# Rotary products and sums and the gate-merge additions on the vector engine instead of POOL

## The chip, the cores and the metric

The kernel runs on one core of one Trainium2 chip. The metric is the device time of one execution in microseconds (us). Before the change three timed runs gave 715.38, 715.96 and 716.66 us; the median is 715.96 us. The engines are named as the profile names them: PE is TensorE (matmul), PEld its weight loads, DVE the vector engine, ACT the scalar engine, POOL is GpSimd, SP the engine whose queue starts the DMA transfers.

## The reference, cut to what matters

One encoder layer over 512 tokens of width 1024, all in float32. A projection of the input gives queries, keys and values of two attention branches, and two sets of gate logits. Branch A is attention with a position bias. Branch B is differential attention, and its queries and keys (512 columns each) are first rotated:

```python
def partial_rope(t, cos, sin):            # the first 16 of each 64 columns
    t1 = t[..., :8]; t2 = t[..., 8:16]
    return concat([t1 * cos - t2 * sin, t1 * sin + t2 * cos, t[..., 16:]])

gates = sigmoid(g + b_gate);  g_a, g_b = split(gates)
merged = g_a * (o_a @ w_branch_a) + g_b * (o_b @ w_branch_b)
x = layer_norm(ALPHA * x + merged @ w_out)            # LN1
x = layer_norm(ALPHA * x + relu(x @ w_ff1)**2 @ w_ff2)  # LN2
```

## The kernel before

Every float32 product is made of three TensorE matmuls. Each operand is split in a high part (ACT casts it, line 84) and a low part (DVE subtracts the high part from the operand, line 85); high by high, high by low and low by high are summed in PSUM. The inner lines of this are L184 to L186 (`tmm`) and L189 to L191 (`smm`). Weights come in chunks of 128x1024 through a ring of three `raw` tiles; the ring parts `wh` and `wl` are the high and the low part.

The program is a generator, `proj()`, for the projections, which is advanced a step at a time between the units of the attention: 32 units of branch A (`attn_a`: 8 heads by 4 query blocks t), then those of branch B (`attn_b`). A unit of branch A computes scores (L275, L276) into one of three PSUM banks called `st`, DVE adds the bias and takes the maximum (L283) and so empties the bank, ACT takes the exponential (L285), POOL divides by the sum (L378, a TENSOR_SCALAR). Three units later PE transposes the result (L294) into another `st` bank, which ACT (L302) and DVE (L303) read into `pq`. The transposes of a unit take the bank from which L283 has just read the scores of the unit before, so PE can't go on until that L283 is done.

While branch A runs, the generator projects the queries and keys of branch B, head by head. `evac_qkb` copies the result to a tile `t` (128x512, called G in the profile, rows are columns of the projection), four small DMAs copy its rotated rows into `other` with the halves exchanged, and `rope` finishes the rotation of the tile before: `other` times the sine table (L500), `t` times the cosine table (L501), then the sum (L502), each over 80 rows and 512 columns. There are eight such tiles. In `prep_b` the rotated tile is split (L259 on ACT, L260 on DVE).

After branch B, `branch(1, ...)` multiplies the attention output by `w_branch_b` in eight groups. Each is scaled by its gate on DVE (L610), added to the same columns of branch A (L613), halved and split (L615 on ACT, L616 on DVE) into `mh` and `ml`. The two halves of `w_out` follow (`s_group`, four chunks of weights each), whose left operands are `mh` and `ml`; DVE adds the result to the input (L821), takes the statistics (L825), and LN1 of each block of 128 rows (L886 to L892) makes the tile that PE transposes (L903). Meanwhile DVE forms sums of blocks of the second MLP weight (L716), whose G tiles are loaded (L779) into buffers that the gates leave. The MLP follows, to the end of the program.

A scheduler sets the order of the instructions on each engine. Each engine works through its own list in order and waits where an operand isn't there. An instruction inside `tc.keep_in_program_order` is pinned: it keeps its place in the program.

Of the kernel before, what the change touches and what calls it, by code (L numbers as in the profile page):

```python
# [13 lines left out]
ALU = mybir.AluOpType  # L14
# [26 lines left out]
def block_kernel(ctx, tc, w, w2, x_t, x, pos, relb, bgate, lq1, lk1, lq2, lk2, subg,  # L41
                 ln1_g, ln1_b, ln1_gt, ln1_bt, ln2_g, ln2_b, out):
    nc = tc.nc
    V, A, G, T = nc.vector, nc.scalar, nc.gpsimd, nc.tensor
# [7 lines left out]
    def name(s):  # L52
        counter[0] += 1
        return f"{s}{counter[0]}"

    def xt(dt=F32):
        return big.tile([P, S], dt, tag="X", bufs=16, name=name("X"))
# [9 lines left out]
    def mm_bank():  # L67
        tag = rotation.pop(0)
        rotation.append(tag)
        return bank(tag)  # L70
# [80 lines left out]
    def chunk(ahead=2):  # L151
        c = next_chunk[0]
        prefetch(c + ahead + 1, c + max(ahead, 1))
        next_chunk[0] += 1
        return parts.pop(c)
# [27 lines left out]
    def tmm(ps, lw_h, lw_l, rh, rl, first, last):  # L183
        T.matmul(ps, lw_h, rh, start=first, stop=False)  # L184
        T.matmul(ps, lw_h, rl, start=False, stop=False)  # L185
        T.matmul(ps, lw_l, rh, start=False, stop=last)  # L186
# [205 lines left out]
    sin_t = tables.tile([P, S], F32, name="sin_t")  # L392
# [85 lines left out]
    def evac_qkb(which):  # L478

        def f(ps):  # L480
            t, o = gt(), other[len(qb[0] + qb[1]) % 2]
            A.activation(t, ps, AF.Copy, scale=0.125 if which == 0 else 1.0)
            for m in (0, 64):
                nc.sync.dma_start(out=o[m:m + 8], in_=t[m + 8:m + 16])
                nc.sync.dma_start(out=o[m + 8:m + 16], in_=t[m:m + 8])
            qb[which].append(t)
            turns.append((t, o))
            if len(turns) > 1:
                rope(*turns.pop(0))
        return f  # L490
# [6 lines left out]

    def rope(t, o):
        r = slice(0, 80)
        tc.keep_in_program_order(G.tensor_tensor(out=o[r], in0=o[r], in1=sin_t[r], op=ALU.mult))  # L500
        V.tensor_tensor(out=t[r], in0=t[r], in1=cos_t[r], op=ALU.mult)  # L501
        G.tensor_tensor(out=t[r], in0=t[r], in1=o[r], op=ALU.add)  # L502

    def prep_b(h):
        if turns:
            rope(*turns.pop())
        q1, k1 = (stack(qb[which][h], 1.0) for which in range(2))
        return q1, [swapped(q) for q in q1], k1
# [88 lines left out]
    def branch(b, oh, ol):  # L597

        for ip in range(4):
            wh, wl = chunk()  # L600
            for j in range(2):
                i = 2 * ip + j
                ps = mm_bank()
                for k in range(4):
                    off = k * 256 + j * 128
                    sl = slice(off % 512, off % 512 + 128)
                    tmm(ps, wh[off // 512][:, sl], wl[off // 512][:, sl], oh[k], ol[k],
                        k == 0, k == 3)
                g, m = gates[8 * b + i], gates[i]
                V.scalar_tensor_tensor(out=g, in0=g, scalar=1.0, in1=ps,  # L610
                                       op0=ALU.add, op1=ALU.mult)
                if b == 1:
                    G.tensor_tensor(out=m, in0=m, in1=g, op=ALU.add)  # L613
                    h, l = xt(FR), xt(FR)
                    A.activation(h, m, AF.Copy, scale=0.5)  # L615
                    V.scalar_tensor_tensor(out=l, in0=m, scalar=0.5, in1=h.bitcast(F32),  # L616
                                           op0=ALU.mult, op1=ALU.subtract)
                    mh.append(h)
                    ml.append(l)
                yield  # L620
# [10 lines left out]
    def proj():  # L631
        def before(c):
            for k in (2 * c + 2, 2 * c + 3):
                if 0 < c and k < KD:
                    load_x(k)
            if c > 1:
                for k in (2 * c, 2 * c + 1):
                    split_x(k)
        yield from s_group(xh, xl, evac_va, before)
        for p in range(4):  # L640
            yield from t_pair(xh, xl, [evac_qk(p, 0), evac_qk(p, 1)])
        for h in range(4):
            yield from t_pair(xh, xl, [evac_qkb(0), evac_qkb(1)])
        yield from s_group(xh, xl, evac_vb)
        for i in range(8):
            yield from t_pair(xh, xl, [evac_gate(i), evac_gate(8 + i)])
        yield from branch(0, oa_h, oa_l)
# [163 lines left out]
    for n, _ in enumerate(branch(1, ob_h, ob_l)):  # L811
        qt.load_next(2)
# [182 lines left out]
    for q in range(4):  # L995
# [24 lines left out]
        if last:  # L1020
            t, p3h, p3l = (late.tile([P, 4, S], dt, tag="x1t", bufs=4, name=name("x1t"))
                           for dt in (F32, FR, FR))
# [148 lines left out]
```

## Time and profile before

| | |
|---|---|
| timed runs | 715.38, 715.96, 716.66 us; median 715.96 us |
| profiled execution | 715.14 us, of which the span from first to last instruction 712.9 us |
| PE busy | 698.0 us (98%), 3259 matmuls |
| DVE busy | 535.7 us (75%), 1016 instructions |
| ACT busy | 383.3 us (54%), 700 instructions |
| POOL busy | 100.7 us (14%), 107 instructions |
| granted TensorE clock | 0.994 (mean of the span) |

The profiled execution's own time is its span and 2.2 us around it. The busy share is a mean over the span; how long a stage lasts is read from the engine that is never idle in it.

### The profile page before, as it was taken

To read this page: it belongs to the slowest core of one execution; us is meant where nothing else is said; L and a number is where in the kernel's file an instruction comes from. 1 tells how busy PE (TensorE), PEld (TensorE's weight loads), DVE (VectorE), ACT (ScalarE), POOL (GpSimd) and SP (SyncE) were. 2 spreads that over 40 slices of the span, in tenths; PEclk is the share of its full clock that TensorE was granted. 3 is DMA by queue.
4 is the path that set the end of the run, shared out by engine and by line. 5 is a ranking of instruction groups with operands and counts; after the bars stand their busy time and mean duration, and the time that the engine had idled before them with its cause. 6 is when DMAs were issued, how large, how long until landed. Compare 5 with 4: busy or idle time off the path is not lost.

```text
span 712.9 us, 9510 instructions
## 1 busy us (share of the span) xinstructions
PE 698.0 (98%) x3259; PEld 580.8 (81%) x3259; DVE 535.7 (75%) x1016; ACT 383.3 (54%) x700; POOL 100.7 (14%) x107
## 2 busy tenths in 40 slices
PE   9999999999999999999999999999999999999993
PEld 6888888888888888888889888888888888888883
DVE  6667668775667676669996898767894779956798
ACT  6556556644667666323556665166623675156610
POOL 2022266740111211034000000000000000000001
PEclk9999999999999999999999999999999999999997
DMA  8554232332333113176542247233640356220403
GB/s 299 209 154 123 95 85 83 111 93 89 93 103 101 59 60 118 60 261 228 189 140 68 89 133 245 66 119 115 214 144 31 117 174 202 68 89 1 148 8 110
DMA packets 36816, 87.27 MB, mean 122 GB/s; under 512 B 5665, under 2 KB 6433, under 8 KB 36769
## 3 DMA queue, kind: packets, MB, share of 16 engines
q1 hardware_dynamic: 36048, 85.72, 37.2%
q10 hardware_dynamic: 720, 0.95, 0.4%
q8 instruction: 25, 0.41, 0.2%
q14 instruction: 23, 0.18, 0.1%
HBM read 79.84 MB, written 2.10 MB: 115 GB/s over the span
## 4 chain that ended last, share of the span: by engine, by line
PE 88%; DVE 5%; ACT 2%; POOL 2%; issue 1%; DMA 1%; SPq 0%; DVEq 0%
PE mm L184 9%; PE mm L186 9%; PE mm L185 9%; PE st L184 6%; PE st L186 6%; PE st L185 6%; PE st L191 4%; PE st L190 4%; PE st L189 4%; PE mm L191 4%; PE mm L190 4%; PE mm L189 4%; PE o L184 2%; PE o L185 2%; PE o L186 2%; POOL G L613 2%
## 5 line engine op out<-in xcount | busy, mean ns | idle before, releaser
L85 DVE TENSOR_TENSOR wl<-raw,wh 128x1024 fp32r<-128x1024 f32 (+1 forms) x86 | 105.0, 1222 | 34.1 <-ACT wh L84 34.1
L84 ACT CAST wh<-raw 128x1024 fp32r<-128x1024 f32 (+1 forms) x86 | 88.5, 1029 | 65.8 <-PE mm L185 23.4
L184 PE MATMUL mm<-X,wh 128*128 128x512 f32 x256 | 103.2, 403 | 0.0
L186 PE MATMUL mm<-X,wl 128*128 128x512 f32 x256 | 100.0, 391 | 0.0
L185 PE MATMUL mm<-X,wh 128*128 128x512 f32 x256 | 99.9, 390 | 0.0
L84 ACT CAST V<-G 128x512 fp32r<-128x512 f32 x104 | 61.6, 619 | 45.2 <-DVE G L716 23.5
L186 PE MATMUL st<-x1t,wl 128*128 128x512 f32 (+1 forms) x200 | 76.2, 381 | 0.0
L185 PE MATMUL st<-x1t,wh 128*128 128x512 f32 (+1 forms) x200 | 76.1, 381 | 0.0
L184 PE MATMUL st<-x1t,wh 128*128 128x512 f32 (+1 forms) x200 | 75.9, 381 | 0.0
L85 DVE TENSOR_TENSOR V<-G,V 128x512 fp32r<-128x512 f32 x104 | 71.2, 697 | 3.1 <-ACT V L84 3.1
L186 PEld LDWEIGHTS mm<-X,wl 128*128 128x128 f32 x256 | 48.1, 188 | 10.5
L184 PEld LDWEIGHTS mm<-X,wh 128*128 128x128 f32 x256 | 48.2, 188 | 8.8
L285 ACT ACTIVATE e<-e,s 128x128 f32<-128x128 f32 (+3 forms) x64 | 36.0, 563 | 36.0 <-DVE s L283 35.2
L185 PEld LDWEIGHTS mm<-X,wh 128*128 128x128 f32 x256 | 48.3, 189 | 8.6
L869 POOL TENSOR_SCALAR s<-s 128x1 f32<-128x1 f32 x1 | 0.4, 411 | 370.9 <-DVE s L853 370.9
L716 DVE TENSOR_TENSOR G<-G,G 128x512 f32<-128x512 f32 x64 | 44.9, 721 | 6.2 <-DMA G<-in_w_dram 6.1
L378 POOL TENSOR_SCALAR e<-e,s 128x128 f32<-128x128 f32 (+3 forms) x32 | 36.7, 1146 | 65.4 <-DVE s L287 61.6
L189 PE MATMUL st<-V,X 128*128 128x512 f32 x116 | 45.3, 391 | 0.0
L190 PE MATMUL st<-V,X 128*128 128x512 f32 x116 | 45.2, 390 | 0.0
L191 PE MATMUL st<-V,X 128*128 128x512 f32 x116 | 45.2, 390 | 0.0
L185 PEld LDWEIGHTS st<-x1t,wh 128*128 128x128 f32 x200 | 37.6, 188 | 7.1
L186 PEld LDWEIGHTS st<-x1t,wl 128*128 128x128 f32 x200 | 37.6, 188 | 7.1
(268 smaller groups left out, 1575.1 us busy)
## 6 DMA issues: line engine op xcount, KB each, us to landing
raw<-in_w_dram SPq DMA_DIRECT2D x86, 512.0 KB
G<-in_w_dram SPq DMA_DIRECT2D x96, 256.0 KB
q<-q SPq DMA_DIRECT2D x32, 128.0 KB
G<-in_relb_dram SPq DMA_DIRECT2D x8, 256.0 KB
x<-in_x_dram SPq DMA_DIRECT2D x4, 512.0 KB
e<-in_x_t_dram SPq DMA_DIRECT2D x7, 256.0 KB
raw<-in_w_dram SPq DMA_DIRECT2D x4, 256.0 KB
out_dram<-x SPq DMA_DIRECT2D x3, 256.0 KB
```

Source lines behind the costliest of these rows:

```text
L84: A.copy(out=h, in_=src)
L85: i = (eng or V).tensor_tensor(out=l, in0=src, in1=h.bitcast(F32), op=ALU.subtract)
L184: T.matmul(ps, lw_h, rh, start=first, stop=False)
L185: T.matmul(ps, lw_h, rl, start=False, stop=False)
L186: T.matmul(ps, lw_l, rh, start=False, stop=last)
L189: T.matmul(ps, ah, w_h, start=first, stop=False)
L190: T.matmul(ps, ah, w_l, start=False, stop=False)
L191: T.matmul(ps, al, w_h, start=False, stop=last)
L285: A.activation(e[:, :n], e[:, :n], AF.Exp, bias=nm, scale=-1.0, accum_out=sums)
L378: G.tensor_scalar(ex[:, :n], ex[:, :n], r, None, op0=ALU.mult)
L613: G.tensor_tensor(out=m, in0=m, in1=g, op=ALU.add)
L716: V.tensor_tensor(out=out, in0=a, in1=b, op=ALU.subtract)
```

## The change

The two rotary operations on POOL go to DVE, and the first loses its pin. The addition in the gate merge goes to DVE.

```diff
     def rope(t, o):
         r = slice(0, 80)
-        tc.keep_in_program_order(G.tensor_tensor(out=o[r], in0=o[r], in1=sin_t[r], op=ALU.mult))
+        V.tensor_tensor(out=o[r], in0=o[r], in1=sin_t[r], op=ALU.mult)
         V.tensor_tensor(out=t[r], in0=t[r], in1=cos_t[r], op=ALU.mult)
-        G.tensor_tensor(out=t[r], in0=t[r], in1=o[r], op=ALU.add)
+        V.tensor_tensor(out=t[r], in0=t[r], in1=o[r], op=ALU.add)
...
                 if b == 1:
-                    G.tensor_tensor(out=m, in0=m, in1=g, op=ALU.add)
+                    V.tensor_tensor(out=m, in0=m, in1=g, op=ALU.add)
```

POOL loses 24 instructions (8 of L500, 8 of L502, 8 of L613), DVE gets 24. PE's list is the same, row by row. The lists of DVE, ACT and SP change order around the moved operations.

On DVE in branch A, at the third of the eight rotations (G_1194; a unit with t = 0 follows), the list changes as follows. L363 reads the attention output, L260 splits the first rotated tile, V_1262 is a low part of that output, e_1289 are the scores that PE waits to have read.

```order
 L85 TENSOR_TENSOR wl_1305<-raw_1146,wh_1304 128x1024
 L287 RECIPROCAL s_1242<-s_1239 128x1
+L500 TENSOR_TENSOR other_99<-other_99,sin_t 80x512
+L363 TENSOR_TENSOR e_1100<-o_1250,e_1100 64x512
 L501 TENSOR_TENSOR G_1194<-G_1194,cos_t 80x512
-L363 TENSOR_TENSOR e_1100<-o_1250,e_1100 64x512
 L260 SCALAR_TENSOR_TENSOR q_1776<-G_1038,q_1776 64x512
-L260 SCALAR_TENSOR_TENSOR q_1779<-G_1038,q_1779 64x512
 L85 TENSOR_TENSOR V_1262<-e_1100,V_1261 128x512
+L502 TENSOR_TENSOR G_1194<-G_1194,other_99 80x512
 L283 ISA e_1289,s_1290<-st_1286,G_429 128x128
```

L500 and L502 now stand ahead of L283, and the second L260 has gone behind it. The seventh rotation (G_1515) has the same change.

On ACT in the gate merge, the list around the cast of the fourth chunk of `w_out` (wh_3487, from raw_3471) changes as follows. V_3433 and V_3434 are casts of the next chunk, raw_3473.

```order
+L615 ACTIVATE X_3425<-G_2981 128x512
+L84 CAST wh_3487<-raw_3471 128x1024
 L84 CAST V_3514<-G_3304 128x512
-L615 ACTIVATE X_3425<-G_2981 128x512
 L84 CAST V_3433<-raw_3473 128x512
-L84 CAST wh_3487<-raw_3471 128x1024
 L84 CAST V_3434<-raw_3473 128x512
```

The cast of the fourth chunk now stands ahead of that of the fifth, no longer behind it.

On DVE, at the end of the first half of `w_out`, the additions of the result (L821, to x_0 to x_3) and the statistics (L825) are now spread between the splits of the last weights (V_3444 to V_3876).

```order
 L85 TENSOR_TENSOR V_3444<-raw_3477,V_3442 128x512
+L821 SCALAR_TENSOR_TENSOR x_0_3210<-x_0_3210,mm_3449 128x512
 L85 TENSOR_TENSOR V_3447<-raw_3479,V_3445 128x512
+L825 BN_STATS bn_3590<-x_0_3210 128x6
+L821 SCALAR_TENSOR_TENSOR x_1_3211<-x_1_3211,mm_3450 128x512
 L85 TENSOR_TENSOR V_3448<-raw_3479,V_3446 128x512
+L825 BN_STATS bn_3599<-x_1_3211 128x6
+L821 SCALAR_TENSOR_TENSOR x_2_3212<-x_2_3212,mm_3451 128x512
+L821 SCALAR_TENSOR_TENSOR x_3_3213<-x_3_3213,mm_3452 128x512
+L825 BN_STATS bn_3612<-x_2_3212 128x6
+L825 BN_STATS bn_3621<-x_3_3213 128x6
 L85 TENSOR_TENSOR V_3876<-G_3408,V_3875 128x512
```

The same eight rows stood behind V_3876 and one L716. The next row in both lists is the L821 of the second half (x_0 from o_3623), with which LN1 of the first row block begins, so the same work stands ahead of it as before, and the L613 besides.

## Rows read from the trace of the kernel before

**Rows 1.** The page's head, and PE's busy tenths in 40 slices of the span.

```profile
span 712.9 us, 9510 instructions
...
PE   9999999999999999999999999999999999999993
```

**Rows 2.** Busy time by window: window, its length, then the named engines.

```profile
320.00:357.00 37.00, 36.94 (x164) 30.27 (x163) 35.24 (x49) 15.94 (x23) 8.37 (x5) 1.00 0.63 209
```

**Rows 3.** Timeline, PE at 114 and 129 us: start, duration, what.

```profile
114.17 0.28 PE L276 MATMUL st<-q,q 128*128 128x256 f32 x1
115.02 0.52 PE L294 MATMUL st<-ident,e 128*128 128x128 f32 x3 [0.57 <-DVE s L283]
...
129.53 0.28 PE L276 MATMUL st<-q,q 128*128 128x256 f32 x1
129.65 0.49 PE L294 MATMUL st<-ident,e 128*128 128x128 f32 x3
```

**Rows 4.** Timeline, DVE from 109 to 115 us.

```profile
109.03 0.69 DVE L501 TENSOR_TENSOR G<-G,cos_t 80x512 f32<-80x512 f32 x1
109.75 0.68 DVE L363 TENSOR_TENSOR e<-o,e 64x512 f32<-64x512 f32 x1
110.47 0.69 DVE L260 SCALAR_TENSOR_TENSOR q<-G,q 64x512 fp32r<-64x512 f32 x1
...
111.19 1.78 DVE L260 SCALAR_TENSOR_TENSOR q<-G,q 64x512 fp32r<-64x512 f32 x1
113.00 1.67 DVE L85 TENSOR_TENSOR V<-e,V 128x512 fp32r<-128x512 f32 x1
114.59 0.28 DVE L283 CUSTOM_DVE_ANT_0 e<-st,G 128x128 f32<-128x128 f32 x1
```

**Rows 5.** Timeline, POOL from 109 to 114 us.

```profile
109.25 1.91 POOL L378 TENSOR_SCALAR e<-e,s 128x512 f32<-128x512 f32 x1 [1.12 <-DVE s L287]
111.13 1.29 POOL L500 TENSOR_TENSOR other<-other,sin_t 80x512 f32<-80x512 f32 x1
112.49 1.62 POOL L502 TENSOR_TENSOR G<-G,other 80x512 f32<-80x512 f32 x1
```

**Rows 6.** Timeline, DVE at the fifth rotation, whose unit PE doesn't wait for.

```profile
126.67 0.29 DVE L283 CUSTOM_DVE_ANT_0 e<-st,G 128x128 f32<-128x128 f32 x1
```

**Rows 7.** Timeline, PE at 342 and 358 us.

```profile
341.42 0.39 PE L191 MATMUL mm<-wh,X 128*128 128x512 f32 x1
341.65 0.39 PE L189 MATMUL mm<-wh,X 128*128 128x512 f32 x1
342.09 0.50 PE L190 MATMUL mm<-wl,X 128*128 128x512 f32 x1
...
358.09 0.39 PE L191 MATMUL st<-V,X 128*128 128x512 f32 x1
359.14 1.06 PE L903 MATMUL mm<-ident,lt 128*128 128x128 f32 x8 [0.66 <-issue]
```

**Rows 8.** Timeline, ACT at 338 us, the cast ahead of that of the fourth chunk.

```profile
338.32 0.62 ACT L84 CAST V<-raw 128x512 fp32r<-128x512 f32 x1 [1.76 <-DMA raw<-in_w_dram]
```

**Rows 9.** Timeline, DVE from 319 to 357 us.

```profile
319.81 1.78 DVE L716 TENSOR_TENSOR G<-G,G 128x512 f32<-128x512 f32 x1
...
322.94 0.68 DVE L716 TENSOR_TENSOR G<-G,G 128x512 f32<-128x512 f32 x1
...
330.11 1.10 DVE L616 SCALAR_TENSOR_TENSOR X<-G,X 128x512 fp32r<-128x512 f32 x1 [1.26 <-ACT X L615]
...
334.68 1.77 DVE L716 TENSOR_TENSOR G<-G,G 128x512 f32<-128x512 f32 x1
...
340.82 1.22 DVE L85 TENSOR_TENSOR wl<-raw,wh 128x1024 fp32r<-128x1024 f32 x1
...
355.78 0.67 DVE L821 SCALAR_TENSOR_TENSOR x<-x,o 128x512 f32<-128x512 f32 x1
```

**Rows 10.** DVE's waits from 305 to 358 us: total, times, longest.

```profile
DVE X L616 <- ACT X L615: 7.2, 4, 2.1
```

## The prediction

> **What bounds the kernel now.** I read the page's head and its slices first: PE is busy for nine tenths or more of every slice but the last [rows 1], and the change leaves PE's list as it is. So no saving on POOL or DVE counts by itself. What can move the end is only the time in which PE stands still, and what the change adds to such pauses. From the page I went to PE's waits, and from these to the timeline of PE at each of them, to see how much later a matmul began than the one before it allows.
>
> Three kinds of pause lie where the change works. First, in branch A: the transposes of a unit begin 0.85 us after the last score matmul began (114.17 to 115.02), where the same pair in an undisturbed unit is 0.12 us apart (129.53 to 129.65) [rows 3]. That is 0.73 us lost. They wait for DVE's L283, which frees the bank. This stands in the trace twice, at the third and the seventh rotation, 30 us apart and with the same numbers. Second, at 342.09 a matmul with `wl` begins 0.44 us after its predecessor, where 0.23 is the pace (341.42 to 341.65) [rows 7]: 0.21 us lost. Third, the first transposes of LN1 begin at 359.14, 1.05 us after the matmul before them, 0.82 more than the pace [rows 7]. Behind `w_out` nothing of the change is left, and PE is the bound to the last slice [rows 1], so what PE gains or loses ahead of it comes out at the end, in full.
>
> **Why DVE was late in branch A.** The queue of DVE ahead of the late L283 runs from 109.03 to 114.59: L501, L363, two L260, one L85 [rows 4]. Two of these take 1.78 and 1.67 us, where their kind takes 0.69. In just that time POOL runs L500 (111.13) and L502 (112.49) [rows 5]. So a two-input operation on POOL holds up a two-input operation on DVE, and costs it some 1.0 us each time; the 1.62 of L502, where L500 beside it took 1.29, shows that it also goes the other way.
>
> **The change in branch A.** It takes both POOL operations away and puts L500 and L502 on DVE, ahead of L283, and one L260 behind it. Ahead of L283 there are then L500, L363, L501, L260, L85, L502: six operations at a pace of 0.72 us (109.03 to 109.75 [rows 4]), 4.32 us together. From 109.03 that gives a start of L283 at 113.35 in place of 114.59. It takes 0.28, and PE began 0.15 after its end before (114.87 to 115.02); so the bank is free for PE at 113.78. PE is ready at 114.17 + 0.12 = 114.29 [rows 3, 4]. The pause goes with 0.5 us to spare: 2 x 0.73 = 1.46 us gained. What is late next there is PE itself. L500 needs the four small DMAs, but L501 writes the tile that these read and waited for them already, so this is no new wait.
>
> Does L378 of POOL, which stays, hold up DVE in the same way? The rows say no: it ran from 109.25 to 111.16, the L260 that began at 110.47 took its plain 0.69 us, and L378 itself was the one that took 1.91 [rows 4, 5]. The Trainium skill says otherwise ("SBUF — State Buffer", Who interferes with whom): a DVE instruction with two SBUF inputs contends with a POOL instruction that reads SBUF, and the second to issue blocks until the first is done. For L260 against L378 this trace doesn't agree: 0.69 us. I go by the row; the case in which L378 does hold up DVE is a rival below.
>
> The other six rotations put the same two operations ahead of, or just behind, an L283 that PE doesn't wait for now. The tightest is the fifth. L283 begins at 126.67 [rows 6]; with two more operations at 0.72 it begins at 128.11 and ends at 128.40, and PE needs it 0.15 ahead of 129.65 [rows 3], so 1.1 us are left. I cost the six at nothing; the cover is that slack. If two DVE operations there were still held up by 1.0 us each, about 0.9 us of pause would arise.
>
> **The change in the merge.** DVE gets eight additions of 0.68 us (the row of L716 at 322.94, the same operation and shape [rows 9]): 5.4 us of work. From 320 to 357 us DVE is busy for 35.24 of 37 us [rows 2], so this isn't free. What it gets back: four operations there took 1.78, 1.77, 1.77 and 1.10 while L613 ran (first and third of the long ones in [rows 9]), 3.7 us more than their plain 0.68 each; and L616 waited 7.2 us in four waits for ACT, which waited for L613 [rows 10]. 1.26 of these lie at 330.11 [rows 9], the other 5.9 between 306 and 320, where DVE has room. With L613 at 0.68 on the same engine, where POOL took 1.3 to 2.2, the chain L610, L613, L615, L616 is shorter by 0.6 to 1.5 us, and the merge's work moves ahead, into that room. The sum lies between +5.4 (nothing comes back) and 5.4 - 3.7 - 7.2 = -5.5 us for the moment at which DVE reaches L821 of the second half. The middle is 0; I take about -1, since 3.7 + 1.26 come back where DVE is full, and of the earlier 5.9 some 1.5 is enough for that.
>
> The pause at 359.14: from L821 at 355.78 to the transposes are 3.36 us [rows 7, 9], and PE is ready at 358.09 + 0.23 = 358.32. L821 must begin by 354.96, 0.82 us earlier. With about -1 this is met; next late is PE. I count 0.82 gained; the ends are -0.82 and +5.4.
>
> The pause at 342.09: `wl` of the fourth chunk is made at 340.82 [rows 9], late because ACT's cast of the same chunk stood behind a cast that waited 1.76 us for the DMA of the fifth chunk [rows 8]. The new order puts it ahead, and the DVE work before it is no longer. 0.21 us gained.
>
> **The sum.** 1.46 + 0.82 + 0.21 = 2.49 us. The profiled execution took 715.14 us (span 712.9 and 2.2 around it), so the changed one 712.65. The median of the timed runs lies 0.82 above the profiled execution: 715.96 - 2.49 = 713.5 us.
>
> **The rivals.**
> Attention only: branch A gains its 1.46, but in the merge the 5.4 us of DVE work eat what comes back, and the pauses at 342 and 359 stay. For it: DVE is full there. Against: 3.7 us of held-up time is written in the rows. 715.96 - 1.46 = 714.5.
>
> L378 blocks: the operation that stays on POOL holds up a two-input DVE operation that comes second. L378 would run to 111.16 as it does now [rows 5], and L501, due at 110.47 behind L500 and L363, would stand still for 0.69. L283 would be done 0.69 later, which gives PE the bank at 114.47, a pause of 0.18 instead of 0.73. Gain 2 x 0.55 + 1.03 = 2.13: 713.8. Against it is the 0.69 of L260, for it the doubled L260 and L85 beside L500 and L502. This is the rule of the Trainium skill's page "SBUF — State Buffer" that was weighed above.
>
> The pauses only move: DVE's new order puts some other wait on PE, of the size of those that go, for example through the fifth rotation. 716.0.
>
> Slower, the full vector engine: in the merge nothing comes back, because the time that DVE stood beside L613 was time it would have spent waiting for W2 loads anyway. Then L821 begins 5.4 us later, all of it is PE's pause at LN1, and with 1.46 gained in branch A the time is 715.96 + 5.4 - 1.46 = 719.9. It decides from the point at which less than 2.5 of the 5.4 us comes back; then the loss exceeds the gain by 1.43. For it: 35.24 of 37 us. The Trainium skill leans the same way ("Perfetto Trace Analysis", Optimizing Scalar/DVE Operations): if DVE is saturated, giving work to another engine, even GpSimd, may make sense; though it adds that between these two it might not help, as they share a read port. The longer durations beside L613 bear out the second half.
>
> **How the numbers follow.** 0.2% is 1.43 us, about what a measurement of this kernel can tell from no change. Chances: forecast 0.50, attention only 0.18, L378 blocks 0.10, pauses only move 0.10, full vector engine 0.12. Attention only lies on the bound and is halved. Faster: 0.50 + 0.10 + 0.09 = 0.69; within: 0.10 + 0.09 = 0.19; slower 0.12. The timed runs lie 0.7 us about their median, so the forecast alone reaches from 712.8 to 714.2. The range goes down to 712.3, for a chain at LN1 and a matmul or two that gain a little more, and up to 716.3, past the pauses that only move; the slower case is left out, and part of the scatter.
>
> **What would show it.** Right: no pause of PE before L294 at the third and seventh rotation; the two L260 and the L85 at 0.69; POOL empty of L500, L502 and L613; every L716 from 319 to 336 at 0.7; L903 of the first row block 0.23 after the matmul before it. Wrong: DVE operations beside L378 that take over 1 us (the rule holds); L283 waited for at the first, fifth or another rotation; L821 of the second half later than 2.7 us after the matmul group whose result it reads, so that PE's pause at LN1 stays or grows. If PE's pauses go and the time doesn't fall, the claim that PE carries them to the end is wrong.

## The result

The changed kernel took 712.61 us (median of six runs, 711.66 to 713.67), the kernel before 716.15 us (715.38 to 716.66) beside it. The ratio is 0.995, with a 95% interval of 0.9937 to 0.9963: faster by half a per cent. The forecast was 713.5. The profiled execution fell from a span of 712.9 to 710.0 us, by 2.9, where the sum of the terms had said 2.49. The medians lie 3.5 apart. The executions of one kernel differ by up to 1.7 us in how their first matmuls run (last section), and the six of the changed kernel are three of 711.66 to 711.82 and three of 713.39 to 713.67: the median, 712.61, lies between the two threes, and no execution took it. The span and the pauses are the better measure of the change.

The head of the page and its first line answer to [rows 1]. PE's busy time is that of before within 1 us; POOL has 24 instructions and 35 us less.

```profile
span 710.0 us, 9485 instructions
...
PE 697.1 (98%) x3259; PEld 580.5 (82%) x3259; DVE 539.8 (76%) x1040; ACT 383.4 (54%) x700; POOL 65.6 (9%) x83
```

PE's timeline at the places of [rows 3] and [rows 7]: start, duration, what.

```profile
114.08 0.28 PE L276 MATMUL st<-q,q 128*128 128x256 f32 x1
114.20 0.49 PE L294 MATMUL st<-ident,e 128*128 128x128 f32 x3
...
339.97 0.39 PE L189 MATMUL mm<-wh,X 128*128 128x512 f32 x1
340.20 0.39 PE L190 MATMUL mm<-wl,X 128*128 128x512 f32 x1
...
356.06 0.39 PE L191 MATMUL st<-V,X 128*128 128x512 f32 x1
356.30 0.93 PE L903 MATMUL mm<-ident,lt 128*128 128x128 f32 x7
```

All three kinds of pause are gone. The transposes follow the scores by 0.12 us, the matmul with `wl` follows at the pace of 0.23, the transposes of LN1 begin 0.24 after the matmul before them. Since PE's list is the same in both kernels, row can be set against row. The changed kernel leads by 0.09 at L276 of the third rotation (114.17 against 114.08) and by 0.82 one instruction later; it leads by 1.68 ahead of the `wl` matmul, 1.89 at it, 2.03 ahead of L903 and 2.84 at L903. Nothing is given back after that.

DVE at the third rotation, answering to [rows 4]:

```profile
108.94 0.69 DVE L500 TENSOR_TENSOR other<-other,sin_t 80x512 f32<-80x512 f32 x1
109.66 0.68 DVE L363 TENSOR_TENSOR e<-o,e 64x512 f32<-64x512 f32 x1
110.37 0.69 DVE L501 TENSOR_TENSOR G<-G,cos_t 80x512 f32<-80x512 f32 x1
111.09 0.68 DVE L260 SCALAR_TENSOR_TENSOR q<-G,q 64x512 fp32r<-64x512 f32 x1
111.81 0.69 DVE L85 TENSOR_TENSOR V<-e,V 128x512 fp32r<-128x512 f32 x1
112.41 0.68 DVE L502 TENSOR_TENSOR G<-G,other 80x512 f32<-80x512 f32 x1
113.02 0.28 DVE L283 CUSTOM_DVE_ANT_0 e<-st,G 128x128 f32<-128x128 f32 x1
```

Six operations at their plain length take less time than the five of before, two of which were held up. L283 comes 1.57 us earlier. In the merge, DVE's window that answers to [rows 2] and the start of LN1 that answers to the last row of [rows 9]:

```profile
320.00:357.00 37.00, 37.00 (x168) 30.69 (x167) 32.94 (x54) 14.09 (x21) 0.00 (x0) 1.00 0.53 172
```

```profile
348.23 0.69 DVE L716 TENSOR_TENSOR G<-G,G 128x512 f32<-128x512 f32 x1
351.05 0.69 DVE L821 SCALAR_TENSOR_TENSOR x<-x,o 128x512 f32<-128x512 f32 x1 [2.13 <-PE o L191]
```

DVE is no longer full there (32.94 of 37 us, before 35.24), and ahead of LN1 it now waits 2.13 us for PE. Before, PE waited for it. The low part of the fourth chunk, which stood at 340.82 in [rows 9], now begins 9.5 us ahead of the `wl` matmul at 340.20:

```profile
330.72 1.22 DVE L85 TENSOR_TENSOR wl<-raw,wh 128x1024 fp32r<-128x1024 f32 x1
```

### The profile page after: what moved, and what is told of

It is laid out like the page before. It is cut to its first block, busy times and chain, and to the rows that moved or that the text cites. A ratio compares the mean times of both kernels' runs of the same rounds, so it can differ in the third digit from the quotient of the medians.

```text
span 710.0 us, 9485 instructions
## 1 busy us (share of the span) xinstructions
PE 697.1 (98%) x3259; PEld 580.5 (82%) x3259; DVE 539.8 (76%) x1040; ACT 383.4 (54%) x700; POOL 65.6 (9%) x83
## 4 chain that ended last, share of the span: by engine, by line
PE 89%; DVE 6%; DMA 3%; ACT 1%; issue 1%; SPq 1%; DVEq 0%
PE mm L184 10%; PE mm L186 10%; PE mm L185 10%; PE st L186 7%; PE st L184 7%; PE st L185 7%; PE mm L191 4%; PE mm L189 4%; PE mm L190 4%; PE st L191 4%; PE st L190 4%; PE st L189 4%; PE o L184 2%; PE o L186 2%; PE o L185 2%; PE st L276 1%
## 5 line engine op out<-in xcount | busy, mean ns | idle before, releaser
L85 DVE TENSOR_TENSOR wl<-raw,wh 128x1024 fp32r<-128x1024 f32 (+1 forms) x86 | 102.8, 1196 | 34.4 <-ACT wh L84 34.4
L85 DVE TENSOR_TENSOR V<-G,V 128x512 fp32r<-128x512 f32 x104 | 70.1, 686 | 3.1 <-ACT V L84 3.1
L716 DVE TENSOR_TENSOR G<-G,G 128x512 f32<-128x512 f32 x64 | 42.8, 687 | 6.2 <-DMA G<-in_w_dram 6.1
L378 POOL TENSOR_SCALAR e<-e,s 128x128 f32<-128x128 f32 (+3 forms) x32 | 39.7, 1240 | 83.4 <-DVE s L287 80.3
L185 PEld LDWEIGHTS st<-x1t,wh 128*128 128x128 f32 x200 | 37.6, 188 | 7.2
L184 PEld LDWEIGHTS st<-x1t,wh 128*128 128x128 f32 x200 | 37.5, 188 | 7.1
```

What stands on the lines that cost most here:

```text
L85: i = (eng or V).tensor_tensor(out=l, in0=src, in1=h.bitcast(F32), op=ALU.subtract)
L378: G.tensor_scalar(ex[:, :n], ex[:, :n], r, None, op0=ALU.mult)
L716: V.tensor_tensor(out=out, in0=a, in1=b, op=ALU.subtract)
```

## The experiments

Where a lead or a lag of PE is given below, it is taken against the changed kernel row by row, as above, since all kernels up to the last experiment have the same list on PE. The edits are shown against the changed kernel.

**The changed kernel again.**

> The changed kernel again, on the same chip as the parts below. The theory: the three places where TensorE stood still are gone (0.73 us at each of two rotations, 0.21 at the fourth chunk of w_out, 0.82 ahead of the first transposes of LN1), so the span is 2.5 to 3.0 us under that of the kernel before. The rival (something else, as a different start or placing, made part of it) expects the pauses to return here in part, or a span that differs from 710.0 by over 1 us.

Median 711.87 us against 716.61 for the kernel before, ratio 0.9939 (0.9922 to 0.9957), span 710.0. No pause returned. By the medians the two kernels lie 4.7 us apart on this chip, by the spans 2.9, and in the last experiment, on another chip, the medians lie 2.1 apart. So below it is the traces, row against row, that tell what a part brings, and not the medians.

**The rotary part alone.**

```diff
-                    V.tensor_tensor(out=m, in0=m, in1=g, op=ALU.add)
+                    G.tensor_tensor(out=m, in0=m, in1=g, op=ALU.add)
```

> Only the rotary products and sums move; the merge addition stays on POOL. The theory expects the two pauses of branch A to be gone and those at the fourth chunk and at LN1 to stay: 1.4 to 1.6 us faster than before. The rival (the merge brought nearly all of it) expects under 0.5 us.

Span 711.3, so 1.6 less than before, as expected; ratio of the timed runs 0.9961 (0.9946 to 0.9976), 713.73 against 716.61 us, which is 2.9 and more than the places explain. The branch A pauses are gone; the two later ones stand as they were, PE losing 0.33 at the `wl` matmul and the one behind it, and 0.81 at LN1, to the changed kernel. PE at LN1:

```profile
356.55 0.39 PE L191 MATMUL st<-V,X 128*128 128x512 f32 x1
357.59 0.63 PE L903 MATMUL mm<-ident,lt 128*128 128x128 f32 x4 [0.65 <-issue]
```

**The merge part alone.**

```diff
     def rope(t, o):
         r = slice(0, 80)
-        V.tensor_tensor(out=o[r], in0=o[r], in1=sin_t[r], op=ALU.mult)
+        tc.keep_in_program_order(G.tensor_tensor(out=o[r], in0=o[r], in1=sin_t[r], op=ALU.mult))
         V.tensor_tensor(out=t[r], in0=t[r], in1=cos_t[r], op=ALU.mult)
-        V.tensor_tensor(out=t[r], in0=t[r], in1=o[r], op=ALU.add)
+        G.tensor_tensor(out=t[r], in0=t[r], in1=o[r], op=ALU.add)
```

> Only the merge addition moves; the rotary operations stay on POOL with their pin. The theory expects the two pauses of branch A to stay and the two later ones to go: 1.0 to 1.3 us faster than before, and this and the rotary part alone to add up to the whole. The rival (DVE is full from 320 to 357 us, so the additions cost what they bring) expects no gain, or a loss, and LN1's pause still there.

Ratio 0.9975 (0.9965 to 0.9984); 714.95 against 716.61 us, 1.7 us where 1.0 to 1.3 was expected. The two pauses of branch A are there, 0.73 us each, and the two later ones are gone. This profile's first matmuls ran slowly (last section), which hides the gain in its span of 712.9. The places add up: branch A 1.46 in its two pauses, and in the merge the 1.17 us by which the kernel before falls back there (1.68 to 2.85), of which this run has nothing. PE's waits, total, times, longest:

```profile
PE st L294 <- DVE s L283: 1.1, 2, 0.6
```

**The rotary operations on POOL, without the pin.**

```diff
-        V.tensor_tensor(out=o[r], in0=o[r], in1=sin_t[r], op=ALU.mult)
+        G.tensor_tensor(out=o[r], in0=o[r], in1=sin_t[r], op=ALU.mult)
         V.tensor_tensor(out=t[r], in0=t[r], in1=cos_t[r], op=ALU.mult)
-        V.tensor_tensor(out=t[r], in0=t[r], in1=o[r], op=ALU.add)
+        G.tensor_tensor(out=t[r], in0=t[r], in1=o[r], op=ALU.add)
```

> The rotary operations stay on POOL but the first loses its pin; the merge addition moves as in the change. If the pin was what hurt in branch A, the two pauses go and the time is that of the changed kernel. The theory says that it is the engine: the two pauses stay, at 0.5 to 0.8 us each, and the time is that of the kernel with only the merge moved.

714.83 us, ratio 0.9994 (0.9984 to 1.0003): the timed runs don't tell it from the kernel before, though its rows show the two later pauses gone. The two pauses of branch A stay, 0.84 and 0.74 us. Without its pin L500 of the third rotation ran 3.5 us earlier on POOL (107.62 in place of 111.13) and held up another operation of DVE, a low part of 128x1024 that took 2.35 us in place of 1.22; L283 came as late as before (114.54). So taking the pin away alone doesn't help. The engine is what counts.

```profile
PE st L294 <- DVE s L283: 1.2, 2, 0.7
```

**The first product on DVE, pinned.**

```diff
-        V.tensor_tensor(out=o[r], in0=o[r], in1=sin_t[r], op=ALU.mult)
+        tc.keep_in_program_order(V.tensor_tensor(out=o[r], in0=o[r], in1=sin_t[r], op=ALU.mult))
```

> As the changed kernel, but with the first product pinned to its place in the program, now on DVE; at the third and seventh rotation the order on DVE then has L500 later and both L260 ahead of L283. If the place is what counts, L283 comes later by one L260 (0.7 us) or has lost what it won; with 0.5 us to spare this would bring a pause of 0.1 to 0.3 us at each of the two places, 0.2 to 0.6 us in all. If only the engine counts, the time is that of the changed kernel.

712.89 us, ratio to before 0.9946 (0.9932 to 0.9961), no pause in branch A: behind the start, where this profile lost 1.6 us, PE keeps its distance to the changed kernel to the end. My expectation that L283 would come later fell. Both L260 stand ahead of it, but L502 has gone behind it, so there are six operations again, and L283 ends 0.9 us ahead of PE's need (114.87 against 115.68 + 0.12 in this trace). DVE's list ahead of L283 is here that of the kernel before [rows 4] with L500 besides: the old order, one operation more, and no pause once POOL runs neither L500 nor L502.

**Unused two-input operations on POOL at the rotations.** Only POOL's list changes. What they write (rows 96 to 127 of `other`) is read by nothing.

```diff
-        r = slice(0, 80)
+        r, u = slice(0, 80), slice(96, 128); [tc.keep_in_program_order(G.tensor_tensor(out=o[u], in0=sin_t[u], in1=cos_t[u], op=ALU.mult)) for _ in range(2)]
```

> The changed kernel, with two unused TENSOR_TENSOR products (32x512, two SBUF inputs) added on POOL at each rotation, behind the L378 that POOL runs there; they write rows that nothing reads. The lists of all other engines stay as they are. The theory (a two-input operation on POOL holds up DVE's two-input operations) expects DVE operations of 1.6 to 1.8 us again at the rotations, and with L283 now behind six operations, pauses of 1.0 to 1.6 us at the third and the seventh: 2 to 4 us slower than the changed kernel. The rival (the pauses went because L283's place in DVE's order changed, not because POOL fell silent) expects no pause and no difference.

718.33 us, ratio to before 1.0039 (1.0024 to 1.0054): slower than before the change. DVE and POOL at the third rotation, then PE:

```profile
112.70 1.67 DVE L85 TENSOR_TENSOR V<-e,V 128x512 fp32r<-128x512 f32 x1
114.30 1.75 DVE L502 TENSOR_TENSOR G<-G,other 80x512 f32<-80x512 f32 x1
115.97 0.28 DVE L283 CUSTOM_DVE_ANT_0 e<-st,G 128x128 f32<-128x128 f32 x1
```

```profile
112.26 3.24 POOL L499 TENSOR_TENSOR other<-sin_t,cos_t 32x512 f32<-32x512 f32 x2
```

```profile
114.11 0.28 PE L276 MATMUL st<-q,q 128*128 128x256 f32 x1
116.40 0.52 PE L294 MATMUL st<-ident,e 128*128 128x128 f32 x3 [2.01 <-DVE s L283]
```

DVE is held up by 1.0 us each by operations that share no data with it, and PE stands still for 2.2 us at the third rotation and 1.3 at the seventh. That settles branch A: DVE's order is that of the changed kernel, and what POOL runs beside it decides. Another 1.6 us were lost to the clock right after the first pause (last section), so this run falls 5.5 us behind the changed kernel, more than the 2 to 4 expected.

The rows also show how long such a hold-up lasts. L502 on DVE ends at 116.05, 0.55 us after the two products on POOL (115.50). In the kernel before, L260 ends at 112.97 and POOL's L500 at 112.42, L85 at 114.67 and L502 at 114.12 [rows 4, 5], again 0.55. Between 90 and 360 us every DVE operation of 512 columns that a TENSOR_TENSOR on POOL held up ends 0.54 to 0.56 us after it, in this run, the kernel before and the runs with unused sums. DVE's operation, the second to start, isn't done until POOL's is; what it loses is about what was left of POOL's operation when it came.

**Unused one-input operations on POOL at the rotations.**

```diff
-        r = slice(0, 80)
+        r, u = slice(0, 80), slice(96, 128); [tc.keep_in_program_order(G.tensor_scalar(o[u], sin_t[u], 2.0, None, op0=ALU.mult)) for _ in range(2)]
```

> As the one before, but the two unused operations on POOL are TENSOR_SCALAR (32x512, one SBUF input), which take as long or longer. My reading of the rows (such a one doesn't hold up DVE; it is itself held up) expects every DVE operation at its plain length and the time of the changed kernel, within 0.3 us. The rule of the Trainium skill, SBUF - State Buffer, Who interferes with whom (a two-input DVE instruction contends with any POOL instruction that reads SBUF, the second to issue waits), expects what it expects of TENSOR_TENSOR: DVE operations of 1.6 us and more, and 2 to 4 us lost.

713.07 us, ratio 0.9961 (0.9948 to 0.9974); no pause in branch A, and the only lag, 1.4 us, arises in the first 11 us of the program. POOL was nearly as busy as before the change (96.3 us, before 100.7), and it was POOL that was held up (two operations 3.60 us, at best 1.49 each). But DVE's operations were not all plain. The low part at the third rotation took 0.99, and POOL ran beside it:

```profile
113.50 0.99 DVE L85 TENSOR_TENSOR V<-e,V 128x512 fp32r<-128x512 f32 x1
```

```profile
112.84 3.60 POOL L499 TENSOR_SCALAR other<-sin_t 32x512 f32<-32x512 f32 x2
```

So my reading was too absolute: a one-input operation on POOL holds DVE up by 0.3 to 0.4 us at times, never by 1.0. The rule that the Trainium skill gives ("SBUF — State Buffer", Who interferes with whom: with two SBUF inputs on DVE and a POOL instruction that reads SBUF, the second to issue blocks) is right that they contend, and for TENSOR_TENSOR the rows above agree that the second waits until the first is done. It is not what these rows show for TENSOR_SCALAR, where L85 began 0.66 us into the first POOL operation (112.84 to 114.83), lost 0.3 and was done at 114.49, before it.

**Unused sums on POOL in the merge, two behind each merge, then one.** `h` is the high part of the merge; `ld` is used no more by then.

```diff
-                    ml.append(l)
+                    ml.append(l); [tc.keep_in_program_order(G.tensor_tensor(out=ld.rearrange("p a b -> p (a b)"), in0=h.bitcast(F32)[:, 0:256], in1=h.bitcast(F32)[:, 256:512], op=ALU.add)) for _ in range(2)]
```

> The changed kernel, with two unused TENSOR_TENSOR sums (128x256) added on POOL behind each of the eight merges; nothing reads what they write, and the other engines' lists stay. They hold up DVE in the stage where it is full, by up to 0.6 us each, some 4 to 9 us in all. The theory that LN1's pause went because the merge no longer waits for POOL, so that DVE works ahead, expects that DVE's spare 2.1 us ahead of LN1 and 1.9 us of PE's take most of this: no pause or under 1 us. The rival, that the pause went because DVE was no longer held up, expects LN1's pause of 0.8 us back or more.

With two: 715.31 us, ratio 0.9992 (0.9981 to 1.0002). PE lost 0.6 us at a matmul that waited for a low part of `w_out`, and 1.6 at LN1. Some 13 operations of DVE took 0.54 us more than their plain length, 7.0 us in all. DVE came to L821 at 356.11:

```profile
323.54 1.22 DVE L616 SCALAR_TENSOR_TENSOR X<-G,X 128x512 fp32r<-128x512 f32 x1
...
356.11 0.68 DVE L821 SCALAR_TENSOR_TENSOR x<-x,o 128x512 f32<-128x512 f32 x1
```

```profile
359.54 1.06 PE L903 MATMUL mm<-ident,lt 128*128 128x128 f32 x8 [1.41 <-issue]
```

My bound of under 1 us fell: 7.0 us are more than DVE can take. They are also twice what L613 had cost it before. So the run was repeated with `range(1)`, one sum behind each merge.

> As the kernel with two unused sums behind each merge, but with one, so that DVE is held up by about half as much, some 3.5 us (two held it up by 7.0), which is what L613 on POOL cost it before the change (3.7 us). The other engines' lists are those of the changed kernel. If being held up made the pause at LN1, it comes back at about its old 0.8 us. If the pause came from the order and the waits (the merge waiting for POOL, DVE's work bunched behind it), DVE absorbs 3.5 us (it waited 2.1 us ahead of LN1, and PE had 1.9 to spare) and there is no pause: a time within 0.3 us of the changed kernel.

713.24 us, ratio 0.9966 (0.9953 to 0.9979), the changed kernel beside it 713.50. Span 711.1 us, and no pause at the fourth chunk or at LN1; the lag of 0.96 us arises in the first 10 us. Seven operations were held up by 0.54, 3.8 us in all, as much as before the change (3.7). L821 and the transposes:

```profile
353.28 0.68 DVE L821 SCALAR_TENSOR_TENSOR x<-x,o 128x512 f32<-128x512 f32 x1
```

```profile
357.03 0.39 PE L191 MATMUL st<-V,X 128*128 128x512 f32 x1
357.26 0.92 PE L903 MATMUL mm<-ident,lt 128*128 128x128 f32 x7
```

So in the merge the held-up time alone doesn't make the pause. With 3.8 us of it and the order and waits of the changed kernel, the pause doesn't come, though DVE reaches L821 with no idle time left. The pause of before needed the merge's wait for POOL, and the DVE work that bunched behind it, as well. That the waits would have made it alone is not shown: L821 was 0.82 us late and the held-up time was 3.7, and no run takes the held-up time away and leaves the merge waiting for POOL.

**More matmuls ahead of the first weights.** Seven matmuls without use run at the start of the program (`warm_up(7)`), while the first weights load; here 8 and 9.

```diff
-    warm_up(7)
+    warm_up(8)
```

> The changed kernel with 8 matmuls before the first weights in place of 7. In some profiles the first matmuls of the program run at 427 ns instead of 227 until 9.8 us, and the times of the changed kernel fall in two groups 1.6 us apart. If the idle 0.5 us of TensorE ahead of its first real matmul is what decides, it shrinks to 0.1 us here, and all executions fall in the lower group, median about 711.8. If it isn't, both groups stay.

> As the one before, with 9 matmuls, which end at about 5.25 us: no idle time ahead of the first real matmul, which starts up to 0.3 us later than it could. If idle time decides, all executions fall in the lower group, 0.3 us above that with 8. If not, both groups stay.

> The changed kernel beside these, for the two groups: some executions near 711.7 and some near 713.4 us, whatever the chip; the pauses stay away in both.

With 8: median 711.91 (711.76 to 712.66), with 9: 711.98 (711.68 to 712.38), the changed kernel beside them 713.50 (712.45 to 713.63). The ratios to the kernel before are 0.9952 (0.9939 to 0.9964), 0.9951 (0.9939 to 0.9964) and 0.9968 (0.9956 to 0.9981). All ten executions with 8 or 9 lie between 711.68 and 712.66, so in this run one or two more such matmuls bring 1.5 to 1.6 us by the medians. The 0.3 us that 9 were to cost didn't appear. The changed kernel beside them didn't do quite what was expected: of its five executions three lie near 713.5, one at 713.03 and the lowest at 712.45, none near 711.7. The trace of the lowest has the quick start, but PE waits in it for input (last section). The pauses stay away in it.

## Why the prediction was right

The bound held: PE's pauses carried the change to the end, 2.75 us of them (2.84 less the 0.09 at the start), in a span that fell by 2.9. The mechanism is as forecast; the time is in part luck. The forecast of 713.5 was built on 2.49 us of pauses and on an offset of 0.82 between a profiled execution and the median, and that offset hangs on how many executions start slowly. Three of six did here. With four quick ones of six the median would have been some 711.8, below the 712.3 to which the range went, as it was on another chip (711.87).

Branch A: 1.46 forecast, 1.59 found between L276 of the third rotation and the `wl` matmul, of which the pauses are 0.73 each and the rest is 0.05 and 0.07 behind them. The cause as given is shown: two-input operations on POOL put it back, one-input operations don't, and neither the pin nor the old order on DVE brings it by itself. The slack that was forecast as 0.5 us was 0.75: L283 ended at 113.30, with the 0.15 of the forecast that is 113.45, and PE was ready at 114.20. The six operations took 4.08 us where the forecast had 4.32, since L502 and L283 each began 0.6 after the operation ahead of it, not 0.72.

L378: the sentence that it does not hold DVE up was too strong. One L501 of the changed kernel took 1.10 us, and one L502 0.78, beside an L378; over 1 us was one of the prediction's own signs of being wrong. It did not matter, as they fell in rotations with room. The rival in which L378 blocks L501 at the third rotation is out (0.69 there).

The fourth chunk: 0.21 forecast, 0.33 found; the matmul behind the `wl` matmul lost 0.11 as well. That the cast's new place on ACT did it is read from the rows, not tested apart from the rest of the merge.

LN1: 0.82 forecast, 0.81 found, though the term behind it was mis-sized. DVE was to reach L821 about 1 us earlier. It was free at 348.92 and began at 351.05, as soon as PE had the result. Set against PE, which by then led by 2.03, that is 2.7 us earlier than before, and DVE was idle 2.1 us longer. Together that is 4.8 us of room, near the far end of the range from +5.4 to -5.5, and the choice of its middle was too cautious: nearly all the waits of L616 [rows 10] came back, 0.7 of the 7.2 us being left, besides the 3.7 us of held-up time, against 5.4 us of added work. PE was next late, as forecast, so the size of it changed nothing. The prediction counted the held-up time first among what comes back; most of the room came from the merge's waits (6.5 us), and the run with one unused sum shows that with these gone the held-up time can stay.

The rivals: "attention only" and "full vector engine" fall with the merge alone, which gained 1.17 us. "The pauses only move" falls with the list of PE's waits, in which none is new.

## What to carry to other kernels

When one engine is busy all the time, set each moment at which it stands still against the pace beside it; those few tenths are all that a change on other engines can win. A two-input operation on POOL can cost its neighbours on DVE about as much as it would cost on DVE itself (here 2.1 us against 1.4 for the two of the third rotation, 3.7 against 5.4 for the eight of the merge), so moving it there may add little to DVE's queue, and it shortens the chain through it. Before putting a gain down to contention, put the contention back alone, with operations that nothing reads, at the size it had. If the loss doesn't return, contention alone wasn't enough; whether it was needed takes a run with the contention away and the rest as it was.

## What the runs showed of the hardware

A pause of PE can cost more than its length. In the run with two-input operations on POOL, PE stood still for 2.2 us from 114 us on, and the granted clock then fell from 1.00 to 0.50 (1.2 of 2.4 GHz) for 3.4 us, from 116.94 to 120.35; eight matmuls ran at 427 ns in place of 227, 1.6 us lost on top. Windows of PE in that run, length, busy time, clock, DMA:

```profile
114.00:116.00 2.00, 0.39 (x3) 1.00 0.09 16
116.00:118.00 2.00, 1.60 (x7) 0.74 0.09 16
118.00:120.00 2.00, 2.00 (x6) 0.50 0.63 240
```

The pause of 1.3 us in this run and those of 0.7 to 1.6 us in the others were not followed by this.

The first matmuls of the program run 427 ns apart in some executions, until 8.9 to 10.2 us. In the profile of the pinned product, two of them, the second the last; in that of the changed kernel, the same matmul as the first of these:

```profile
6.35 0.63 PE L191 MATMUL mm<-wh,X 128*128 128x512 f32 x1
...
9.77 0.63 PE L191 MATMUL mm<-wh,X 128*128 128x512 f32 x1
```

```profile
6.05 0.39 PE L191 MATMUL mm<-wh,X 128*128 128x512 f32 x1
```

In both, PE had run seven matmuls at that pace and then stood still for half a microsecond. It costs 1.1 to 1.7 us in the four profiles that have it, which fits executions near 711.8 and near 713.4 us. A view of these windows prints a granted clock of 1.00 in both, but that is no reading: the trace's clock records, all of 1.00 at first, begin only at 10.39 us in the pinned product and at 4.40 in the changed kernel, and the view counts time without a record as 1.00. In the four profiles with a slow start (the pinned product, the merge alone, the one-input operations, the two sums) the records begin between 9.13 and 10.39 us, within 0.4 us of where the matmuls quicken, in the ten others between 3.90 and 6.11. The spacing of 427 ns is that of the matmuls above at 0.50, so the slow start looks like the lower level of the clock, held longer; no record shows the level itself. With 8 or 9 matmuls ahead, which leave PE idle for 0.2 us or none, no execution of ten took over 712.66 us; whether idle time or the number of matmuls decides stays open. Part of the scatter is another thing: in two profiles at full pace PE waited 0.7 to 0.9 us at 8 us for the second tile of the input.
